# Sparse attention: value products of a pair's two heads on the two column halves of TensorE, compressed values as one product

## The chip, the core and the metric

One NeuronCore of one Trainium2 chip runs the whole program in one launch. The metric is the device time of that launch in microseconds (us). TensorE (PE) multiplies; its weight loads are shown as an engine of their own (PEld). VectorE (DVE), ScalarE (ACT) and GpSimd (POOL) work on the elements, and SyncE (SP) issues most of the DMAs.

## What is computed

The reference is a long chain of two blocks on 512 tokens of 1024 numbers: mixed attention and an expert layer in the first, a gated convolution and a sparse attention in the second. The change lies in the sparse attention at the end. Cut to that:

```python
p_c = masked_softmax(s_c, m_c)                       # over 31 compressed blocks
o_c = jnp.einsum('bqgin,bngd->bqgid', p_c, v_cmp)
...
p_s = masked_softmax(...)                            # selected blocks: 16 of 8, so all of them, causal
o_s = jnp.einsum('bqginl,bqgnld->bqgid', p_s, vg)
...
p_w = masked_softmax(s_w, m_w)                       # window of 512
o_w = jnp.einsum('bqgik,bkgd->bqgid', p_w, vw)
return g[..., 0:1] * o_c + g[..., 1:2] * o_s + g[..., 2:3] * o_w
...
y = o.reshape(B, S, ATTN_D) * jax.nn.silu(z)
return x + y @ w_out                                 # then a last norm
```

There are 16 heads of 64 in 4 groups of keys and values. With 512 tokens both the selected blocks and the window come to plain causal attention with keys and values of their own, two "branches".

## The kernel before

`phase_nsa` (from L1354) makes keys, values, compressed values, queries and gates, and then calls `attend` (L1632), where the change lies. Behind it comes the output product with `b_out` and the last norm.

`attend` works on pairs of heads: m is one of 8 pairs, which is 128 rows of the output, 64 for each head i. A job is (m, qb, i), with qb one of the four blocks of 128 queries in the order `QB = (3, 0, 2, 1)`; there are 64 jobs. Each passes through four steps, which `pipeline` records one job apart: `f_s` the scores of both branches (L1650 to L1652, the last being the mask as a bf16 product), `f_p` the softmax (maximum on DVE in L1662 or L1665, exponential on ACT in L1668, the sums' reciprocals and the scaling on DVE in L1669 to L1672), `f_t` the transposes on PE (L1681) and their copy to SBUF into `aT` on ACT (L1684), and `f_o` the products with the values (L1696, L1700).

`f_o` adds all terms of a pair into one PSUM bank `o` of 128 rows by 512 queries. A product of L1700 has 128 rows of keys, 64 columns of values and 128 queries, all in fp32, and writes 64 of the 128 rows of `o`: the lower half for i = 0, the upper for i = 1, which is also the half of the PE's columns on which it runs. Job (m, qb, i) has 2 (qb + 1) of these, all on one half. There are 320 of them in all, and each is two PE instructions in the trace (an fp32 product is made in two). Before the first of a pair's block stands L1696, the compressed values: 64 rows (two heads of 32 compressed keys each, and 32 pairs of pcT rows by the parity of m), 128 columns, 128 queries; 32 of these. When the last block of m is done, DVE multiplies `o` by the gate (L1704).

The names `s`, `pt`, `o` and `z` are banks of PSUM: four, two, one and one. The first stretch of `attend` has the last three of the gate's products (`z`, L178 to L180) laid between its jobs. The order on each engine is not the recorded one: a scheduler places the instructions by its own estimates, and each engine then runs its queue in order.

The compressed values `vbd` are laid out in `small_values` (L1489): four copies of 32 partitions each into a zeroed tile (L1366).

Of the kernel before, what the change touches and what calls it, by code (L numbers as in the profile page):

```python
# [10 lines left out]
F32 = mybir.dt.float32  # L11
# [7 lines left out]
PSUM = bass.MemoryType.PSUM  # L19
# [9 lines left out]
ND = 384  # tokens that go through all experts; the others fetch theirs  # L29

# how much of the work in the background is laid beside a unit of products, by part
# [4 lines left out]
# depths of the buffers  # L36
# [3 lines left out]
# where the products of a part turn to halves of the tokens, or are laid behind other work  # L40
# [4 lines left out]
# orders  # L45
# [12 lines left out]
class Ctx:  # L58
    """What all parts share: the core, the pools, the constants and the stream of weights."""
# [76 lines left out]
    def in_turn(self, op, prev=None):  # L136
        """Queue op behind prev, or behind the split that was traced last."""
        self.tc.add_manual_dep(op.ins, (prev or self.last).ins.name,
                               mybir.DependencyInfo(mybir.DependencyClass.NoSync, mybir.DependencyReason.DATA),
                               reason="pace")  # L140
# [41 lines left out]
    def gemm_w(self, key, out, act, k0=0, start=True, stop=True, pump=3.0):  # L182
        """out[m, t] (+)= sum over k of w[k, m] act[k, t] for one unit of weights."""
# [6 lines left out]
    def gemm_halves(self, jobs, act, done=None, after=None):  # L190
        """gemm_w on each half of the tokens in turn; jobs: (out, its units, each with its first k)."""
# [17 lines left out]
    def gemm_t(self, keys, outs, act, N, pump=3.0):  # L209
        """outs[tb][t, n] = sum over k of act[k, t] w[k, n]; keys: (unit, its first k, its count of k)."""  # L210
# [10 lines left out]
    def halves(self, hi, lo, src):  # L221
        """hi + lo = src exactly, each short enough for one pass."""
# [8 lines left out]
class Modulation:  # L231
    """silu(c) @ ada_w + ada_b, a sixth of its columns at a time, each a sum over rows and then partitions."""
# [33 lines left out]
def bcast(ap, n):  # L266
    """A row of DRAM on n partitions."""
    return bass.AP(tensor=ap.tensor, offset=ap.offset, ap=[[0, n]] + list(ap.ap))
# [33 lines left out]
class Norm:  # L302
    """1 / sqrt(mean of x^2 + eps) of each token, over all partitions; x [d, t] with d on partitions.

    The squares are summed with tokens on partitions, so that the root and its reciprocal (with a step of
    Newton's) take few elements, and brought back along the diagonal of a product."""
# [51 lines left out]
    def whole(self):  # L358
        """For all tokens at once, the squares summed by products."""
# [21 lines left out]
    def bare(self, k, g, act):  # L381
        """act = halves of x * g, their products to be scaled by r."""
# [7 lines left out]
def pipeline(n, stages, bg=None):  # L390
    """Emit stage s of job j at step j + s: later stages of earlier jobs first."""
# [10 lines left out]
# ================================================================ first block, mixing part  # L402
def phase_a(c, xres, mod):
    tc, nc, a = c.tc, c.nc, c.a
    with tc.tile_pool(name="pa", bufs=1) as pool, ExitStack() as scope, ExitStack() as pscope:
        psp = pscope.enter_context(tc.tile_pool(name="psa", bufs=7, space=PSUM))
        psm = pscope.enter_context(tc.tile_pool(name="psm", bufs=1, space=PSUM))
# [100 lines left out]
        def rotate(dsts, x, tab, tb, G):  # L508
            """x * cos + swap(x) * sin on G heads of 64."""
# [13 lines left out]
        def vt(keys, N, act_in):  # L523
            """A product with tokens on partitions."""
# [10 lines left out]
        def transposes(src, nblk, put):  # L535
            """src(b): [t, 128] to transpose; put(b0, n, psum) takes up to four of them."""
# [164 lines left out]
        # lambda  # L701
# [185 lines left out]
class Act:  # L887
    """The input of the products; its room is lent to the raw weights when it isn't needed."""
# [10 lines left out]
class Banks:  # L899
    """The eight banks of PSUM, taken in turn, or by the names that they are divided by."""  # L900
# [20 lines left out]
# ================================================================ experts  # L921
# [5 lines left out]
def phase_peer(c, xres, xscope, mod):  # L927
    """x += g2 * (sum over the chosen experts of gate * gelu(u . h) v).

    The first ND tokens go through all experts as products, their gates laid out over all experts (zero where  # L930
    an expert isn't chosen); the other tokens fetch the rows of their experts."""
# [10 lines left out]
    with ExitStack() as gscope, ExitStack() as psc, ExitStack() as vscope, ExitStack() as hscope, \  # L942
# [42 lines left out]
        def top16(vals, idx, src, tmp):  # L985
            """The 16 largest of a row, largest first, the earlier first among equals, and their places."""
# [89 lines left out]
        def gates(tb):  # L1076
            """The gate of every expert for each token: the sum over slots of one-hot x one-hot."""
# [35 lines left out]
        def gather():  # L1113
            """The experts of the tokens from ND on, a slot of all of them at a time."""
# [165 lines left out]
# ================================================================ second block: gated convolution  # L1280
# [72 lines left out]
# ================================================================ second block: attention  # L1353
# [499 lines left out]
```

## Time and profile before

| | us |
|---|---|
| median of 3 runs (2503.88 to 2516.2) | 2514.8 |
| span of the profiled execution, first to last instruction | 2495.9 |
| of it: attention, first product of `attend` to the last of L1700 | 222.4 |
| of it: from there to the end | 49.2 |

The span is the part of the profiled execution that the trace shows; what the launch takes around it is in the median of the runs alone. A record of a PE instruction starts when it is dispatched and ends when its results are written, so records overlap: the distance from one start to the next is what an instruction takes of the engine's time, and the chain of the profile is cut in just these distances. A line names the code, `o<-aT,V` is the tile written and the tiles read, and `128*64 128x128` is the rows and columns of the array and the moving operand.

### The profile page before, as it was taken

To read this page: it belongs to the slowest core of one execution; us is meant where nothing else is said; L and a number is where in the kernel's file an instruction comes from. 1 tells how busy PE (TensorE), PEld (TensorE's weight loads), DVE (VectorE), ACT (ScalarE), POOL (GpSimd) and SP (SyncE) were. 2 spreads that over 40 slices of the span, in tenths; PEclk is the share of its full clock that TensorE was granted. 3 is DMA by queue.
4 is the path that set the end of the run, shared out by engine and by line. 5 is a ranking of instruction groups with operands and counts; after the bars stand their busy time and mean duration, and the time that the engine had idled before them with its cause. 6 is when DMAs were issued, how large, how long until landed. Compare 5 with 4: busy or idle time off the path is not lost.

```text
span 2495.9 us, 37763 instructions
## 1 busy us (share of the span) xinstructions
PE 2461.3 (99%) x13725; PEld 2215.4 (89%) x13725; DVE 1861.5 (75%) x4173; ACT 1150.6 (46%) x2354; POOL 356.1 (14%) x332
## 2 busy tenths in 40 slices
PE   7999999999999999999999999999999999999998
PEld 4875788999999999999999999988888888887777
DVE  7885489999999878778888887765555456766654
ACT  3566443434777858633333333422222333545652
POOL 0000000014334333224332222000000010000000
PEclk8998999999999999999999999999999999999999
DMA  7560152468989998899999998332222352220002
GB/s 269 149 212 1 43 196 77 156 236 307 332 313 322 366 348 320 289 373 354 358 352 340 349 327 294 94 99 96 96 98 94 101 176 84 77 68 18 1 1 77
DMA packets 170939, 490.48 MB, mean 197 GB/s; under 512 B 15473, under 2 KB 62513, under 8 KB 169089
## 3 DMA queue, kind: packets, MB, share of 16 engines
q1 hardware_dynamic: 123744, 295.48, 34.3%
q0 software_dynamic: 44992, 189.68, 20.8%
q10 hardware_dynamic: 2016, 2.91, 0.4%
q8 instruction: 109, 1.79, 0.3%
q14 instruction: 78, 0.63, 0.1%
HBM read 437.15 MB, written 50.86 MB: 196 GB/s over the span
## 4 chain that ended last, share of the span: by engine, by line
PE 87%; DVE 5%; DMA 3%; issue 3%; POOL 1%; ACT 0%; SPq 0%; DVEq 0%; POOLq 0%; ACTq 0%
PE s L180 8%; PE s L179 8%; PE s L178 8%; PE mm L180 6%; PE mm L178 6%; PE mm L179 6%; PE pt L178 4%; PE pt L180 4%; PE pt L179 4%; PE gp L1081 3%; PE o L1700 3%; PE z L178 2%; PE z L180 2%; PE z L179 2%; PE o L180 2%
## 5 line engine op out<-in xcount | busy, mean ns | idle before, releaser
L102 ACT ACTIVATE whi<-wraw 128x1024 fp32r<-128x1024 f32 (+2 forms) x292 | 305.2, 1046 | 547.1 <-PE mm L179 167.2
L103 DVE TENSOR_TENSOR wlo<-wraw,whi 128x1024 fp32r<-128x1024 f32 (+2 forms) x292 | 350.6, 1202 | 97.7 <-ACT whi L102 96.0
L179 PE MATMUL mm<-act,whi 128*128 128x384 f32 (+2 forms) x1176 | 402.2, 343 | 0.0
L180 PE MATMUL mm<-act,wlo 128*128 128x384 f32 (+2 forms) x1176 | 401.5, 343 | 0.2
L178 PE MATMUL mm<-act,whi 128*128 128x384 f32 (+2 forms) x1176 | 398.9, 342 | 0.7 <-DVE xres L844 0.7
L102 ACT ACTIVATE whi<-act 128x1024 fp32r<-128x1024 f32 x126 | 133.5, 1060 | 324.9 <-issue 314.0
L180 PEld LDWEIGHTS mm<-act,wlo 128*128 128x128 f32 x1176 | 221.4, 188 | 5.4 <-DVE wlo L103 1.5
L179 PEld LDWEIGHTS mm<-act,whi 128*128 128x128 f32 x1176 | 221.4, 188 | 3.9
L178 PEld LDWEIGHTS mm<-act,whi 128*128 128x128 f32 x1176 | 219.8, 188 | 4.8 <-issue 0.8
L103 DVE TENSOR_TENSOR wlo<-act,whi 128x1024 fp32r<-128x1024 f32 x126 | 154.1, 1224 | 82.5 <-ACT whi L102 81.2
L1117 POOL DMA_INDIRECT ug<-in_peer_u_rows_dram,eiG x128 | 155.6, 1216 | 374.7 <-DVE ug L1125 258.9
L1117 POOL DMA_INDIRECT vg<-in_peer_v_rows_dram,eiG x128 | 158.6, 1239 | 295.6 <-DVE yG L1135 193.0
L179 PE MATMUL s<-w_lo,whi 128*128 128x384 f32 x512 | 171.1, 334 | 0.9 <-DVE w_lo L224 0.9
L178 PE MATMUL s<-w_hi,whi 128*128 128x384 f32 x512 | 170.3, 334 | 0.6 <-ACT ga L1191 0.6
L180 PE MATMUL s<-w_hi,wlo 128*128 128x384 f32 x512 | 170.5, 334 | 0.0
L1135 DVE SCALAR_TENSOR_TENSOR yG<-vg,gG,yG 128x1024 f32<-128x1024 f32 x127 | 162.2, 1277 | 7.4 <-DMA vg<-in_peer_v_rows_dram,eiG 7.2
L1125 DVE SCALAR_TENSOR_TENSOR ug<-ug,hG 128x1024 f32<-128x1024 f32 x128 | 155.4, 1217 | 8.7 <-DMA ug<-in_peer_u_rows_dram,eiG 8.6
L180 PE MATMUL s<-act,wlo 128*128 128x512 f32 x344 | 134.0, 390 | 0.2 <-DVE wlo L103 0.2
L178 PE MATMUL s<-act,whi 128*128 128x512 f32 x344 | 134.2, 391 | 0.0
L179 PE MATMUL s<-act,whi 128*128 128x512 f32 x344 | 133.6, 389 | 0.0
L1095 DVE TENSOR_SCALAR oh<-iof,idxT 128x128 f32<-128x128 f32 x384 | 116.7, 348 | 8.3 <-PE gp L1081 8.1
L1081 PE MATMUL gp<-oh,oh 128*128 128x128 f32 x768 | 115.0, 274 | 0.0
(676 smaller groups left out, 5810.4 us busy)
## 6 DMA issues: line engine op xcount, KB each, us to landing
wraw<-in_peer_u_dram SPq DMA_DIRECT2D x128, 512.0 KB, 5.3
act<-in_peer_v_rows_dram SPq DMA_DIRECT2D x126, 512.0 KB, 6.6
wraw<-in_a_in_dram SPq DMA_DIRECT2D x64, 512.0 KB, 3.3
Ad<-ga POOLq DMA_DIRECT2D x30, 768.0 KB, 8.2
ga<-Ad SPq DMA_DIRECT2D x30, 768.0 KB, 9.1
Gd<-gc POOLq DMA_DIRECT2D x10, 2048.0 KB, 10.2
gg<-Gd SPq DMA_DIRECT2D x32, 640.0 KB, 7.4
wraw<-in_ada_w_dram SPq DMA_DIRECT2D x32, 512.0 KB, 4.3
```

Source lines behind the costliest of these rows:

```text
L102: self.first = first = self.nc.scalar.activation(hi[:, :n], r[:, :n], AF.Copy)
L103: self.last = self.nc.vector.tensor_tensor(lo[:, :n], r[:, :n], hi[:, :n].bitcast(F32), op=OP.subtract)
L178: mm(out, lh, rh, start=start, stop=False)
L179: mm(out, lh, rl, start=False, stop=False)
L180: self.product = mm(out, ll, rh, start=False, stop=stop)
L1081: nc.tensor.matmul(gp[:, j, :], o1, o2, start=True, stop=True)
L1095: nc.vector.tensor_scalar(o1, iof, idxT[:, 0, t:t + 1], idxT[:, 2, t:t + 1], op0=OP.is_equal, op1=OP.mult)
L1117: nc.gpsimd.indirect_dma_start(out=t, out_offset=None, in_=tab, in_offset=bass.IndirectOffsetOnAxis(ap=eiG[:, j:j + 1], axis=0))
L1125: c.in_turn(nc.vector.scalar_tensor_tensor(u, u, 1.0, hG, op0=OP.mult, op1=OP.mult, accum_out=aG[:, j:j + 1]))
L1135: op = nc.vector.scalar_tensor_tensor(yG, v, gG[:, j:j + 1], yG, op0=OP.mult, op1=OP.add)
L1700: nc.tensor.matmul(o[rr, t], V[:, b, br * 256 + g * 64:br * 256 + (g + 1) * 64], ws[br][:, b * P:(b + 1) * P], start=False, stop=i == 1 an ...
```

## The change

`f_o` now does nothing for i = 0 but keep the transposed weights of the job; for i = 1 it issues the products of both heads, one of head 0, one of head 1 in turn. The ring `aT` has five tiles instead of four. The compressed values of a pair m are one product of 128 rows by 512 queries, whose weights `vbd[:, m % 2, g, :]` are zero in the rows that belong to the pair of the other parity; it opens the whole bank. `vbd` is zeroed and filled at the start of `attend` from a small tile `vsm`, which is one copy in `small_values`.

```diff
-        vbd = pool.tile([P, 4, P], F32, name="vbd")
+        vsm = pool.tile([P, 4, 64], F32, name="vsm")
         nc.gpsimd.memset(kbd, 0.0)
-        nc.gpsimd.memset(vbd, 0.0)
...
-            for q in range(4):
-                rr = slice(32 * q, 32 * q + 32)
-                cc = slice(64 * (q % 2), 64 * (q % 2) + 64)
-                nc.vector.tensor_copy(vbd[rr, :, cc], vv[rr, :, :])
+            nc.vector.tensor_copy(vsm, vv)
...
+    vbd = pool.tile([P, 2, 4, P], F32, name="vbd")
+    nc.gpsimd.memset(vbd, 0.0)
+    for q in range(4):
+        rr = slice(32 * q, 32 * q + 32)
+        nc.vector.tensor_copy(vbd[rr, q // 2, :, 64 * (q % 2):64 * (q % 2) + 64], vsm[rr, :, :])
...
-        ws, w1 = both(pool, "aT", n, bufs=4)
+        ws, w1 = both(pool, "aT", n, bufs=5)
...
     def f_o(j, ws):
         m, qb, i = jobs[j]
+        if i == 0:
+            held[m, qb] = ws
+            return
         g = m // 2
         t = slice(qb * P, (qb + 1) * P)
-        if i == 0 and qb == QB[0]:
+        if qb == QB[0]:
             O[m] = psp.tile([P, S], F32, name="o")
-        o = O[m]
-        if i == 0:
-            rr = slice(64 * (m % 2), 64 * (m % 2) + 64)
-            nc.tensor.matmul(o[:, t], vbd[rr, g, :], pcT[rr, g, t], start=True, stop=False, skip_group_check=True)
-        rr = slice(64 * i, 64 * i + 64)
+            nc.tensor.matmul(O[m], vbd[:, m % 2, g, :], pcT[:, g, :], start=True, stop=False, skip_group_check=True)
+        o, pair = O[m], (held.pop((m, qb)), ws)
         for br in range(2):
+            v = slice(br * 256 + g * 64, br * 256 + (g + 1) * 64)
             for b in range(qb + 1):
-                nc.tensor.matmul(o[rr, t], V[:, b, br * 256 + g * 64:br * 256 + (g + 1) * 64], ws[br][:, b * P:(b + 1) * P],
-                                 start=False, stop=i == 1 and br == 1 and b == qb, skip_group_check=True)
-        if i == 1 and qb == QB[-1]:
+                for h in range(2):
+                    nc.tensor.matmul(o[64 * h:64 * h + 64, t], V[:, b, v], pair[h][br][:, b * P:(b + 1) * P],
+                                     start=False, stop=br == 1 and b == qb, skip_group_check=True)
+        if qb == QB[-1]:
```

In the changed kernel's numbering the scores are L1651 to L1653, the transposes L1682, the compressed product L1700 and the value products L1706. On PE, at the turn to the third pair (m = 2), the queue before:

```order
L1681 MATMUL pt<-ident,aP 128x128 x4
L1696 MATMUL o<-pcT,vbd 128x128
L1700 MATMUL o<-aT,V 64x128 x8
L1650 MATMUL s<-Khi,Q 128x384
L1651 MATMUL s<-Klo,Q 128x384
L1652 LDWEIGHTS identb
L1652 MATMUL s<-maskb,identb 128x128
L1700 MATMUL o<-aT,V 64x128 x4
L1681 MATMUL pt<-ident,aP 128x128 x2
```

and the same place now:

```order
L1700 MATMUL o<-pcT,vbd 128x512
L1706 MATMUL o<-aT,V 64x128
L1682 MATMUL pt<-ident,aP 128x128 x8
L1651 MATMUL s<-Khi,Q 128x384
L1652 MATMUL s<-Klo,Q 128x384
L1653 LDWEIGHTS identb
L1653 MATMUL s<-maskb,identb 128x128
L1706 MATMUL o<-aT,V 64x128 x8
L1682 MATMUL pt<-ident,aP 128x128 x2
```

The 16 products of the block's two heads come in runs of 1, 8 and 7 now, where head 0 had one run of 8 and head 1 two of 4. Over all of `attend` the 320 products stand in 88 runs before and in 79 now; other work comes directly behind a run, or behind L1696, 95 times before, and 78 times behind a run now.

Inside a run the two heads alternate, which the tiles' numbers show; this is a run of 7 in the fifth pair (on PE, now):

```order
L1706 MATMUL o_22750<-aT_22730,V_20268 64x128
L1706 MATMUL o_22750<-aT_22697,V_20268 64x128
L1706 MATMUL o_22750<-aT_22730,V_20268 64x128
L1706 MATMUL o_22750<-aT_22697,V_20268 64x128
L1706 MATMUL o_22750<-aT_22730,V_20268 64x128
```

`aT_22697` holds head 0 and `aT_22730` head 1 of one block of queries; each row is two instructions in a trace. On DVE the four copies into `vbd` now stand at the start of `attend`, between the first maxima and the first sums:

```order
L1666 TENSOR_REDUCE amx<-s 128x1 x3
L1635 COPY vbd<-vsm 32x4x64 x4
L1670 RECIPROCAL asm<-asm 128x2
L1671 TENSOR_TENSOR asm<-asm,gates 128x2
L1673 TENSOR_SCALAR aP<-aP,asm 128x512 x2
```

Before, the reciprocal stood directly behind the three maxima. POOL's zeroing of `vbd` moved with them, behind the last weights of the small network and ahead of the DMAs that bring back `xres` for the output.

## Rows read from the trace of the kernel before

**Rows 1.** The page: the span, and PE's busy time, share and instructions.
```profile
span 2495.9 us, 37763 instructions
PE 2461.3 (99%) x13725; PEld 2215.4 (89%) x13725; DVE 1861.5 (75%) x4173; ACT 1150.6 (46%) x2354; POOL 356.1 (14%) x332
```

**Rows 2.** Busy time by stretch: length, then PE, PEld, DVE, ACT, POOL, clock, DMA.
```profile
2224.30:2446.70 222.40, 222.40 (x1519) 173.64 (x1518) 128.99 (x374) 123.86 (x367) 0.00 (x0) 1.00 0.03 11
2446.70:2495.90 49.20, 38.85 (x285) 36.31 (x285) 27.13 (x62) 14.44 (x28) 4.27 (x8) 0.94 0.29 97
```

**Rows 3.** The same view for one pair m in the middle of the attention.
```profile
2307.71:2332.26 24.55, 24.55 (x178) 19.26 (x177) 15.43 (x46) 14.77 (x47) 0.00 (x0) 1.00 0.00 1
```

**Rows 4.** Who waited for whom, 2224 to 2447: us in total, times, longest.
```profile
ACT aT L1684 <- PE pt L1681: 87.4, 76, 5.8
DVE amx L1662 <- PE s L1652: 30.6, 23, 1.9
...
PEld L1652 <- issue: 13.6, 63, 0.3
...
PEld o L1700 <- ACT aP L1668: 0.4, 1, 0.4
```

**Rows 5.** Groups by line, 2200 to 2450: busy us, mean ns, idle before and releasers.
```profile
L1700 PE MATMUL o<-aT,V 128*64 128x128 f32 x640 | 88.7, 280 | 0.0
L1700 PEld LDWEIGHTS o<-aT,V 128*64 128x64 f32 x640 | 67.5, 136 | 9.0 <-issue 3.0 <-ACT aP L1668 0.4
```

**Rows 6.** The chain of work, 2340 to 2352: start us, us, what.
```profile
2340.39 1.02 PE o L1700 x8
2341.41 0.58 PE pt L1681 x4
2342.00 0.18 PE s L1650
...
2344.46 0.45 PE pt L1681 x4
...
2345.77 0.42 PE o L1696 x2
2346.19 1.89 PE o L1700 x16
2348.08 0.37 PE s L1650
```

**Rows 7.** The chain at 2191: an fp32 product of 128 rows and 512 columns.
```profile
2191.45 0.86 PE o L1421 x2
```

**Rows 8.** PEld in order of time, the same run's weight loads, two and three of them.
```profile
2311.50 0.19 PEld L1700 LDWEIGHTS o<-aT,V 128*64 128x64 f32 x2
...
2311.50 0.30 PEld L1700 LDWEIGHTS o<-aT,V 128*64 128x64 f32 x3
```

**Rows 9.** PE in order of time, the products of these loads, one and two.
```profile
2311.51 0.32 PE L1700 MATMUL o<-aT,V 128*64 128x128 f32 x1
...
2311.51 0.43 PE L1700 MATMUL o<-aT,V 128*64 128x128 f32 x2
```

**Rows 10.** The zeroing of `vbd` and its copies: ns min/median/max, starts.
```profile
L1366 POOL MEMSET vbd<- x1: 525/525/525, 2028.8 to 2028.8; 128x512 f32 x1
...
L1489 DVE COPY vbd<-s x4: 406/420/429, 2130.7 to 2132.0; 32x256 f32<-32x256 f32 x4
```

**Rows 11.** DVE in order of time at the start of `attend`, and PE's first transposes.
```profile
2227.38 1.89 DVE L1665 TENSOR_REDUCE amx<-s 128x1 f32<-128x512 f32 x3
2229.64 0.17 DVE L1669 RECIPROCAL asm<-asm 128x2 f32<-128x2 f32 x1 [0.38 <-ACT aP L1668]
...
2233.55 0.88 PE pt L1681 x8
```

**Rows 12.** The chain behind the last value product.
```profile
2445.65 1.03 PE o L1700 x8
2446.70 1.07 ACT s L102
```

More of the change, by code (lines that the diff above doesn't have):

```diff
@@ L1599, in phase_nsa @@
         with tc.tile_pool(name="nsx", bufs=1) as p1:
-            attend(c, p1, psp, Q, Khi, Klo, V, vbd, pcT, gates, sz, gate)
+            attend(c, p1, psp, Q, Khi, Klo, V, vsm, pcT, gates, sz, gate)
         nscope.close()
@@ L1629, in phase_nsa, with attend @@
         qscope.close()
-def attend(c, pool, psp, Q, Khi, Klo, V, vbd, pcT, gates, sz, gate):
+def attend(c, pool, psp, Q, Khi, Klo, V, vsm, pcT, gates, sz, gate):
     nc = c.nc
     jobs = [(m, qb, i) for m in range(KD) for qb in QB for i in range(2)]
+    vbd = pool.tile([P, 2, 4, P], F32, name="vbd")
[3 more added lines that the diff above has]
+        nc.vector.tensor_copy(vbd[rr, q // 2, :, 64 * (q % 2):64 * (q % 2) + 64], vsm[rr, :, :])
     O = {}
@@ L1685, in f_t @@
         return ws
+    held = {}
     def f_o(j, ws):
         m, qb, i = jobs[j]
+        if i == 0:
+            held[m, qb] = ws
+            return
         g = m // 2
         t = slice(qb * P, (qb + 1) * P)
-        if i == 0 and qb == QB[0]:
+        if qb == QB[0]:
             O[m] = psp.tile([P, S], F32, name="o")
-        o = O[m]
-        if i == 0:
-            rr = slice(64 * (m % 2), 64 * (m % 2) + 64)
-            nc.tensor.matmul(o[:, t], vbd[rr, g, :], pcT[rr, g, t], start=True, stop=False, skip_group_check=True)
-        rr = slice(64 * i, 64 * i + 64)
+            nc.tensor.matmul(O[m], vbd[:, m % 2, g, :], pcT[:, g, :], start=True, stop=False, skip_group_check=True)
+        o, pair = O[m], (held.pop((m, qb)), ws)
         for br in range(2):
+            v = slice(br * 256 + g * 64, br * 256 + (g + 1) * 64)
             for b in range(qb + 1):
-                nc.tensor.matmul(o[rr, t], V[:, b, br * 256 + g * 64:br * 256 + (g + 1) * 64], ws[br][:, b * P:(b + 1) * P],
-                                 start=False, stop=i == 1 and br == 1 and b == qb, skip_group_check=True)
-        if i == 1 and qb == QB[-1]:
+                for h in range(2):
+                    nc.tensor.matmul(o[64 * h:64 * h + 64, t], V[:, b, v], pair[h][br][:, b * P:(b + 1) * P],
+                                     start=False, stop=br == 1 and b == qb, skip_group_check=True)
+        if qb == QB[-1]:
             y = pool.tile([P, S], F32, name="y", bufs=2)
```

## The prediction

> **What bounds the kernel now.** I read the page first: PE is busy for 99% of the span, no other engine over 75% [rows 1]. A mean over such a long program says little of one stage, so I cut the attention out by stretches: for 222.40 us, from its first score product to its last value product, PE is busy without a gap, at a granted clock of 1.00, while DVE has 128.99 us of work and ACT 123.86 [rows 2]. One pair m in the middle takes 24.55 us, with 15.43 of DVE and 14.77 of ACT [rows 3]. Busy PE need not be PE that sets the pace, so the waits come next: ACT waits 87.4 us for the transposes, DVE 30.6 for scores, and PE waits for nobody, but for 0.4 us in all; what is left of its idle time is "issue", 0.3 us at the longest [rows 4]. So the stage lasts as long as PE's queue takes to run. The next instructions behind it hang on its end: a split of `b_out` on ACT begins at 2446.70, when the last value products have ended [rows 12]. What the stage gains should reach the end of the program.
>
> **What an instruction takes.** A group's mean of 280 ns [rows 5] is a record's length, not its cost. The chain gives costs: a run of 8 value instructions takes 1.02 us and one of 16 takes 1.89, so 8 more cost 0.87, which is 0.109 each; 1.02 less 8 x 0.109 leaves 0.15 for each run, whatever its length [rows 6]. The work behind a run pays too: four transposes take 0.58 behind value products and 0.45 behind scores, 0.13 more, and a score product takes 0.37 where it otherwise takes 0.18 [rows 6]; I take 0.14. So going to a run of half-array products and back costs 0.29, about 0.145 each way. The compressed product pays the same twice over: L1696's 128 columns take 0.42 [rows 6], of which two instructions of 0.107 stream, if an fp32 product of 512 columns takes 0.86 [rows 7] and so 0.215 for 128.
>
> **The change part by part.**
>
> 1. *Fewer switches.* The runs go from 88 to 79, which is 9 x 0.15 = 1.3 us less. The 32 products of L1696 cost 32 x 0.42 = 13.4 us; the 8 that replace them have 128 rows and 512 columns, 0.86 each by [rows 7], 6.9 us, and need no switch: 6.5 us less. Returns to the whole array go from 95 to 78: 17 x 0.14 = 2.4 us less. Together 10.2 us, all of it in PE's queue, with nothing beside it. This needs no overlap and comes whatever the next part does. The multiplied zeros cost nothing, since 8 x 512 columns stream as long as 32 x 128.
>
> 2. *Two halves in turn.* Now 640 instructions take 640 x 0.109 = 69.8 us. No row shows two products on different halves next to each other, so this is bounded from both sides. Best: the second instruction of one head's product streams beside the first of the other's. A run of n products then takes n + 1 steps of 0.109 instead of 2n, and the saving is (320 - 79) x 0.109 = 26.3 us. Worst without a new cost: no overlap, 0. Between them: the loads. A load's record is 0.136 long and a product's 0.28 [rows 5]. The second load of a run begins 0.054 behind the first (0.19 less 0.136) and the third 0.164 behind it (0.30 less 0.136) [rows 8], just when the second product has begun, at 0.15 (0.43 less 0.28) [rows 9]. So a load goes out when the instruction ahead of it has started, and on one half it is then hidden. If the load for the other half also waits for that start, each change of half shows these 0.053 or so and a product of two instructions takes 0.109 + 0.053 = 0.162 instead of 0.218: 241 x 0.056 = 13.5 us. Below zero: if each change of half is paid like a switch of shape, 241 x 0.145 = 35 us are lost. I take the best end: the two streams need different columns, different rows of `o` and different tiles `aT`, the weights of the other half are free to be loaded, and the tie of load to start in [rows 8] is seen only where the half in question is in use.
>
>    [...]
>
> 3. *The start of `attend`.* POOL zeroes `vbd`, twice the size of the old one, 0.53 us for that [rows 10], so some 1.05. The only thing behind it on POOL are the DMAs of `xres`, which wait for the end of the attention anyway. Then DVE makes four copies, 4 x 0.42 = 1.7 us [rows 10], behind the first three maxima and ahead of the first sums. DVE's first sums waited 0.38 for ACT, and the scaled weights are done at about 2231, while PE's first transposes begin at 2233.55 [rows 11]: 1.3 us later is still in time. The compressed product waits for these copies, and stands ahead of the first transposes. Cost 0, up to 1.7 if the zeroing is late. In `small_values` three copies (1.3 us of DVE) go from a stretch in which PE is full; 0.
>
> 4. *What holds the products back.* The lower head's weights wait for the upper's, and `aT` has five tiles, of which a pair of the larger blocks takes four. In the order the earlier pair's products stand ahead of every transpose that reuses their tiles, so this is 0 on paper. But the gain brings DVE and ACT nearer to PE: 36.5 us less is 4.6 per pair, 20.0 of 24.55, and DVE is then busy for 15.43 / 20.0 = 77% and ACT for 74%. They still fit, but the handoffs that PE never waited for get shorter, and the order was made by estimates that I don't know. I take 3.5 us for waits that appear (a tenth of the gain; a choice). From 0 to 8.
>
> **Sum.** 10.2 + 26.3 - 3.5 = 33 us. The profiled span goes from 2495.9 to about 2463. The median of the runs is 18.9 over the span and the lowest 8.0 [rows 1], so I carry the difference over: 2514.8 - 33 = 2482 us.
>
> **The rivals.**
>
> A. *Loads aren't pulled ahead.* The halves overlap only in part, for what [rows 8] shows on one half holds across halves. 10.2 + 13.5 - 2 for waits = 22 us: 2493 us. For it: the load always leaves just behind the start of the instruction ahead. Against: that is also what two places for weights per half would give.
>
> B. *The change doesn't do what it says.* PE's queue is strict and a product waits for the one ahead, half or no half: only the switches go. 10 us: 2505 us; if also every change of half shows a load, 241 x 0.053 = 12.8 are lost and it is 2517. For it: no record here shows two products streaming at once. Against: nothing but the absence.
>
> [...]
>
> [...]
>
> **How the numbers follow.** Forecast 0.43, A 0.27, B 0.20, C 0.10. A measurement of this kernel tells about 0.5% from no change, 12.6 us; the three runs of before are 12.3 us apart. Faster by more than that: the forecast, A, and few cases of B with luck in the order: 0.74. Within: most of B, and C where its price is small: 0.17. Slower: 0.09. The range has to take in the forecast, with no waits at 2514.8 - 36.5 = 2478 and some room for the spread of the runs below it, A at 2493, and the main case of B at 2505: 2475 to 2506 leaves out C and the worse half of B, a little under 0.2.
>
> **What the profile of the changed kernel would show.** In a run of 7 or 8 value products the chain or the starts: 0.109 per product (two instructions) for the forecast, 0.162 for A, 0.218 for B, 0.36 for C. The stretch of the attention at about 190 us for the forecast, 201 for A, 212 for B. Runs of one product at some 0.37 (two instructions of 0.109 and 0.15). The compressed product at 0.86, eight of them. Waits of PE for `aP`, `aT` or for maxima that were not there before, some us in all: over 10 would say that part 4 was too small and that DVE or ACT took over. PE waiting at the first compressed product for `vbd` would say that part 3 was wrong. A stretch behind the attention that isn't 49 us would say that the gain does not pass through to the end.

## The result, and the profile after

The changed kernel takes 2465.2 us (median of 4 runs, 2458.9 to 2476.5) beside 2514.6 us for the kernel before (4 runs, 2503.9 to 2516.2): a ratio of 0.9836, 95% interval 0.9808 to 0.9864. It is faster, as forecast, but the time lies below the range of 2475 to 2506. So the question is where some 17 us more than the 33 of the sum came from.

The profiled execution of the changed kernel has a span of 2467.7 us and took 2469.45. The stretches of the attention and of what follows, in the columns of [rows 2] (length, then busy time of PE, PEld, DVE, ACT and POOL, granted clock, DMA):

```profile
2230.00:2416.20 186.20, 186.20 (x1476) 138.12 (x1474) 126.14 (x378) 122.07 (x367) 0.95 (x1) 1.00 0.04 13
2416.20:2467.70 51.50, 39.63 (x283) 37.26 (x282) 27.10 (x62) 14.42 (x28) 4.27 (x8) 0.90 0.27 93
```

From the first score product to the end of the last value product the attention went from 222.30 us (the window of [rows 2] is 0.1 wider) to 186.18, 36.1 less, and PE is busy for all of it, as in [rows 2]. DVE and ACT have the work they had, now 68% and 66% of the stretch. Who waits for whom in it, in the columns of [rows 4]:

```profile
ACT aT L1685 <- PE pt L1682: 54.1, 57, 4.2
DVE amx L1666 <- PE s L1653: 19.9, 32, 3.5
DVE amx L1663 <- PE s L1653: 15.2, 20, 1.8
...
PEld o L1706 <- ACT aP L1669: 1.5, 6, 0.4
```

ACT and DVE still wait for PE (54.1 us where it was 87.4 in [rows 4]). In the other direction only weight loads wait, 3.2 us in all, of which the last row is the largest; PE itself has no gap. What a run of value products takes is read from the chain of work, as in [rows 6] (start, us, engine, tile, line, count of instructions, two of which are a product):

```profile
2284.71 0.81 PE o L1706 x12
...
2286.66 0.80 PE o L1706 x10
...
2290.02 1.02 PE o L1706 x14
...
2292.52 0.91 PE o L1700 x2
...
2295.24 1.02 PE o L1706 x16
...
2404.39 0.36 PE o L1706 x2
...
2415.19 1.03 PE o L1706 x14
2416.25 1.07 ACT s L102
```

The ends of PE's records are modelled by the profile, so no row shows when results are written, and the pieces of a chain run from one end to the next, not from start to start; for a whole run it comes to the same: in the first row the 12 start at 2284.64, and what follows them starts at 2285.45. Sixteen instructions take 1.02 us, as eight did in [rows 6], and 14 take the same. The last row is the split of `b_out` on ACT, which begins at the attention's end as in [rows 12].

That two products stream at once is seen in the rows of PE in order of time. These are three answers for one run, cut 0.03, 0.26 and 0.37 us after its start; a row counts what had started by the cut:

```profile
2264.47 0.33 PE L1706 MATMUL o<-aT,V 128*64 128x128 f32 x2
...
2264.47 0.44 PE L1706 MATMUL o<-aT,V 128*64 128x128 f32 x4
...
2264.47 0.55 PE L1706 MATMUL o<-aT,V 128*64 128x128 f32 x6
```

Where single instructions followed each other in [rows 9], pairs do now. In the records of this run the two of a pair start 6 or 7 ns apart.

**What the 17 us are.** The runs of the kernel before, 70 more of them beside the experiments, have a median of 2504.7 us (2495.1 to 2519.9); only 9 of the 70 are at 2514.4 or above, where three of the first four lay. The 70 come from four chips, whose medians lie between 2503 and 2506, so it is not the chip that makes the difference, as far as is known (that of the first runs is not on record). Twenty runs of the changed kernel have a median of 2468.8 us (2456.1 to 2477.9). In every run the time is its span plus 1.7 to 1.85 us. The distance to the forecast is then: 10.1 us because the median of the three runs it started from was that much above the median of many, 2.9 because the gain is 35.9 us and not 33, and 3.6 because the first four runs of the changed kernel were that much below their own median of many; 16.6 in all.

The spread of a kernel's runs follows the granted clock. At a mean clock of 0.987 to 0.989 the spans of before average 2495.6 us (24 runs), at 0.983 to 0.985 2503.8 (24), at 0.979 to 0.981 2512.8 (22); those of the changed kernel 2458.8 (7), 2468.0 (9) and 2474.5 (4). The difference is 36 to 38 us at each level. Where the clock is lost is seen in the first fifth of the program. The stretch from 180 to 240 us in the trace of before, in the columns of [rows 2]:

```profile
180.00:240.00 60.00, 60.00 (x257) 34.89 (x257) 32.84 (x90) 37.22 (x136) 0.00 (x0) 0.77 0.03 9
```

the same in that of the changed kernel:

```profile
180.00:240.00 60.00, 60.00 (x194) 32.15 (x193) 27.56 (x77) 30.06 (x112) 0.00 (x0) 0.60 0.03 9
```

and in that of `e4_turn_only`, one of the experiments below:

```profile
180.00:240.00 60.00, 60.00 (x166) 31.92 (x166) 25.56 (x71) 27.21 (x103) 0.00 (x0) 0.53 0.03 9
```

The instructions up to there are the same in all three, yet PE got through 257, 194 and 166 of them. In the trace of before the clock is 0.50 from 184 to 208 us and 1.00 from 210 to 240, in that of the changed kernel 0.50 from 182 to 228 and 1.00 from 229 to 240. If it has only these two values in the stretch, a mean of 0.77 is 27.6 us at 0.50 and the rest at 1.00; 0.60 is 48 us, and 0.53 is 56.4 us with more to come. In each of the three PE had been idle for 0.69 us at 177 us, waiting for ACT, and some 3 to 5 us later the clock fell: it is 0.68 from 180 to 182 us in the changed kernel, and 0.55 and 0.63 from 182 to 186 in the other two. In the chain of the changed kernel that wait is

```profile
176.71 0.25 PE ps L180
176.96 0.02 issue
176.98 0.61 ACT act L531
177.59 0.04 issue
177.63 0.49 PE s L734 x2
```

The gap goes with the fall, but it does not explain it. At 285 us PE waits 1.41 us for DVE, twice as long, and the clock stays at 1.00, here in the changed kernel:

```profile
280.00:300.00 20.00, 18.51 (x101) 15.56 (x100) 9.73 (x13) 11.13 (x21) 0.00 (x0) 1.00 0.24 78
```

It is so in the six profiles that have these stretches, the two of before, two of the changed kernel, `e3_no_turn` and `e4_turn_only`: from 120 to 180 us PE is idle for 0.69, from 180 to 200 the clock is 0.50 to 0.58, and in the 20 us that hold the longer gap, between 260 and 300, PE is idle for 1.49 and the clock is 1.00. How long it stays down differs: 27.6, 48 and over 60 us in the three traces, in which the attention starts at 2224.4, 2230.0 and 2239.6 us.

### The profile page after: what moved, and what is told of

The parts are those of the page before. It is cut to its first block, busy times and chain, and to the rows that moved or that the text cites. A ratio compares the mean times of both kernels' runs of the same rounds, so it can differ in the third digit from the quotient of the medians.

```text
span 2467.7 us, 37681 instructions
## 1 busy us (share of the span) xinstructions
PE 2432.1 (99%) x13677; PEld 2183.5 (88%) x13677; DVE 1857.9 (75%) x4174; ACT 1149.0 (47%) x2354; POOL 354.0 (14%) x332
## 4 chain that ended last, share of the span: by engine, by line
PE 93%; DMA 3%; DVE 3%; issue 0%; ACT 0%; SPq 0%; DVEq 0%; ACTq 0%
PE mm L178 8%; PE mm L180 8%; PE mm L179 8%; PE s L180 8%; PE s L179 8%; PE s L178 8%; PE pt L178 4%; PE pt L180 4%; PE pt L179 4%; PE gp L1081 3%; PE z L178 2%; PE z L179 2%; PE z L180 2%; PE o L1706 2%; PE o L178 2%; PE o L179 2%
```

## The experiments

The attention's length, from its first score product to the end of its last value product, turned out to be independent of the clock's draw earlier on: 222.30 us in both profiles of the kernel before, 186.17 to 186.18 in four of the changed kernel. So it is the number to compare; the ratio of the whole stands beside it. Ratios are against runs of the kernel before in the same rounds. "Steps" is worked out from the queue: in each run, twice the number of products on the half that has more of them. That is what a run takes if the halves overlap fully, as they do not in `e10_one_then_other` (28.5 steps for a run's 16, below).

| kernel | runs of products | steps | attention, us | median, us (runs) | ratio to before, 95% interval |
|---|---|---|---|---|---|
| before | 88 | 640 | 222.30 | 2504.7 (70) | 1 |
| changed | 79 | 384 | 186.18 | 2468.8 (20) | see below |
| `e3_no_turn` | 95 | 634 | 217.14 | 2497.8 (10) | 0.9974 (0.9949 to 0.9998) |
| `e4_turn_only` | 80 | 384 | 195.54 | 2486.0 (6) | 0.9924 (0.9888 to 0.9960) |
| `e5_whole_runs` | 50 | 356 | 174.24 | 2456.7 (5) | 0.9803 (0.9778 to 0.9828) |
| `e7_by_two` | 81 | 448 | 193.62 | 2475.7 (4) | 0.9871 (0.9844 to 0.9899) |
| `e8_fixed_steps` | 34 | 324 | 201.78 | 2490.7 (6) | 0.9915 (0.9885 to 0.9945) |
| `e9_last_first` | 32 | 320 | 167.50 | 2456.4 (6) | 0.9797 (0.9757 to 0.9837) |
| `e12_last_first_again` | 32 | 320 | 167.51 | 2449.6 (6) | 0.9792 (0.9767 to 0.9817) |
| `e10_one_then_other` | 32 | 320 | 189.88 | 2472.2 (4) | 0.9865 (0.9820 to 0.9911) |

**The two kernels again.** `e1_after_again` is the changed kernel, `e2_before_again` the kernel before.

> The changed kernel again, beside the kernel before. Theory (the attention gained 36.4 us, 222.40 to 186.00, and the rest of the difference between the first medians, 49.5 us, is a granted clock that fell early in the program in some executions): at one mean granted clock the two spans differ by 36 to 38 us, the medians by 34 to 45, and the attention lasts 186 us again. Rival (the change gains some 12 us more somewhere outside the attention): the spans differ by 47 to 50 us also where the mean clocks are equal. Second question: what lies around the span. Theory: each run is its span plus 1.7 to 1.8 us, so 2459 to 2475. Rival, the one the prediction carried: 8 to 19 us over the span.

> The kernel before against itself. Theory: the same, ratio 1.000 within 0.004; its spans lie between 2495 and 2515 and follow the mean granted clock, 0.01 of clock being some 20 to 25 us, and the time is the span plus 1.75 us in each run. The attention lasts 222.4 us whatever the clock did earlier. Rival (the profiled execution of before, 2495.9, is a thing of the profiler, and runs without it need 2503 or more at the same clock): spans of 2503 to 2515 at a mean clock of 0.988.

The changed kernel: attention 186.18 us, median 2470.4, ratio 0.9864 (0.9828 to 0.9900); at clocks of 0.988 and 0.989 its spans were 2461.8 and 2454.4, on average some 37 below those of before at that clock. The medians differ by 33.0, a little less than the 34 to 45 that were expected. The kernel before against itself: 1.0011 (0.9984 to 1.0038), attention 222.30, spans 2494.4 to 2517.1 with the clock from 0.989 down to 0.979, each 1.7 to 1.8 us below its time. So there is no gain elsewhere, and the profiled execution of before was an ordinary one with a high clock.

Two later repeats asked whether the change itself moves the clock.

> The changed kernel a third time, on the chip and in the rounds of the two kernels above. Theory: the attention lasts 186.2 us again; the start of the attention lies at 2221 to 2240 us, the later the lower the mean granted clock (2222 at 0.988, 2230 to 2235 at 0.984), and the time is that start plus 186.2, plus 49 to 52 for the rest, plus 1.75. Rival (the change itself lowers the clock): starts at 2230 and later in all its runs, where those of before stay at 2224.

> The changed kernel in the same rounds. Theory: the attention lasts 186.2 us, the ratio to before is 0.985 to 0.986 where the clocks are drawn alike ((2504.7 - 36.1) / 2504.7 = 0.9856), and the kernel with 32 whole runs lies 18 to 19 us below it. Rival (clocks differ by kernel): a ratio outside 0.983 to 0.988.

They gave 0.9833 (0.9790 to 0.9876) and 0.9862 (0.9836 to 0.9888), attention 186.18 and 186.17. The four profiled executions of the changed kernel all have a clock of 0.983 or 0.984 and begin the attention at 2228.9 to 2235.0, which alone would suit the rival. But over all runs the mean clock is 0.9846 (20 runs) beside 0.9843 for before (70), and 7 of the 20 have 0.987 or more, as 24 of the 70 do. So the rival falls: the clock's draw is not the change's doing. One of these expectations was missed by a little: the kernel with 32 whole runs (below) lies 19.7 us under `e13_after_fourth` by the medians, for 18 to 19.

**Without the turn.** All products of head 0, then all of head 1:

```diff
-        for br in range(2):
-            v = slice(br * 256 + g * 64, br * 256 + (g + 1) * 64)
-            for b in range(qb + 1):
-                for h in range(2):
+        for h in range(2):
+            for br in range(2):
+                v = slice(br * 256 + g * 64, br * 256 + (g + 1) * 64)
+                for b in range(qb + 1):
```

> As the changed kernel, but a block's products are issued all of head 0, then all of head 1, so that a change of half comes once in a run, not at every product. Theory (the two streams overlap only where neighbours are on different halves): a run of n products takes 2n steps of 0.109 us, less one where it changes half, so about 26 us of the gain are lost; the queue has 95 runs here against 79, which at 0.29 each adds some 4.6: the attention lasts 213 to 217 us, +26 to +31 us against the changed kernel, -5 to -10 against before. Rival (the gain comes from the merged block, the larger compressed product and the fifth tile of aT, and not from the turn): the attention stays at 186 to 192 us.

The attention took 217.14 us, 30.96 more than the changed kernel, at the upper end of what was expected, and 5.16 less than before. In its queue a run stays on one half, with one exception, and the chain shows what that costs:

```profile
2300.95 0.58 PE o L1706 x4
...
2304.15 0.80 PE o L1706 x6
...
2311.70 0.36 PE o L1706 x2
```

Six instructions take 0.80 us here; in the changed kernel twelve do. The turn is the change's main part, and the rival that credits the rest falls.

**Only the turn.** The compressed values as before, 32 products of 64 rows with the old layout of `vbd`:

```diff
-            nc.tensor.matmul(O[m], vbd[:, m % 2, g, :], pcT[:, g, :], start=True, stop=False, skip_group_check=True)
+        rr = slice(64 * (m % 2), 64 * (m % 2) + 64)
+        nc.tensor.matmul(O[m][:, t], vbd[rr, g, :], pcT[rr, g, t], start=True, stop=False, skip_group_check=True)
```

> As the changed kernel, but the compressed values as before: 32 products of 64 rows, one per block of a pair, with the tile vbd laid out as before; the heads still go in turn. Theory: the 8 large products cost 8 x 0.86 = 6.9 us where the 32 cost 32 x 0.42 = 13.4, and each of the 32 that is followed by other work pays a return of 0.14: +7 to +10 us, the attention at 193 to 196, about -27 us against before. Rival (the small product, on 64 of the 128 rows, also breaks the pairing of the two heads behind it, or the array's shape goes through more states): +12 us or more. Other rival (the switch is paid once per run in any case, and the small product opens a run that would be opened anyway): +0 to +3 us.

195.54 us, 9.36 more: within the 7 to 10, so both rivals fall. Its median, 2486, says little, since four of its six runs drew a clock of 0.979 to 0.981; the one at 0.987 has a span of 2466.5, 7.7 above the mean of the changed kernel's seven at 0.987 to 0.989.

**Every second change of half.** Two products of one head, then two of the other:

```diff
-        for br in range(2):
-            v = slice(br * 256 + g * 64, br * 256 + (g + 1) * 64)
-            for b in range(qb + 1):
-                for h in range(2):
+        todo = [(br, b) for br in range(2) for b in range(qb + 1)]
+        for k in range(0, len(todo), 2):
+            for h in range(2):
+                for br, b in todo[k:k + 2]:
+                    v = slice(br * 256 + g * 64, br * 256 + (g + 1) * 64)
```

> The changed kernel, but the heads change after every two products, not after every one: two of head 0, two of head 1, and so on; 81 runs. Theory (only the instructions next to a change of half stream beside each other, and one change hides one step of 0.109): a run of n products then shows about 88 hidden steps in all instead of 241, so 16.7 us of the overlap are lost and some 0.8 for two runs more: the attention at 203 to 204 us. Rival (the two halves are queues of their own, and PE runs ahead on the one while the other is busy, so the grain of the turn doesn't matter): 186 to 190 us. Other rival (only a strict alternation pairs at all): 213 to 217, as with no turn.

193.62 us, 7.4 more and not 16.7: the theory that each change hides one step falls. The chain:

```profile
2316.80 0.58 PE o L1707 x4
...
2318.00 1.07 PE o L1707 x16
...
2320.11 1.02 PE o L1707 x12
```

Sixteen instructions in blocks of four by half take 1.07 us, nearly as in strict turn (1.02). As I read it, PE does not keep to the order of its queue here: it passes the instructions that wait for the busy half and starts those of the free one. The run of 16, cut 0.07 us after its start, has two instructions under way, and the four at its head are all of one half:

```profile
2317.93 0.34 PE L1707 MATMUL o<-aT,V 128*64 128x128 f32 x2
```

The row with 12 is four products on one half and two on the other: 0.15 + 8 x 0.109 = 1.02, the fuller half alone. What the kernel loses are runs of two products of one head, 31 of them, at 0.58: in all 64 steps more, 64 x 0.109 = 7.0 us, and two runs. The rival of two queues was right in kind; its 186 to 190 had not counted those runs.

**How far PE gets ahead.** The kernel with whole runs (below), but in each run all products of head 1 and then all of head 0:

```diff
-        for br in (1, 0):
-            v = slice(br * 256 + g * 64, br * 256 + (g + 1) * 64)
-            for b in range(qb + 1):
-                for h in (1, 0):
+        for h in (1, 0):
+            for br in (1, 0):
+                v = slice(br * 256 + g * 64, br * 256 + (g + 1) * 64)
+                for b in range(qb + 1):
```

> As the kernel with 32 whole runs, but inside a run all products of head 1 come first and then all of head 0, so that there is one change of half in a run. It asks how far PE gets ahead on one half while the other is busy. Theory 1 (each half is a queue without a bound that matters here): a run of 16 products lasts 1.9 us as with the turn, and the attention 165 us. Theory 2 (PE looks past a few instructions only; two products, four instructions, were passed in the kernel that changes by two): in each run four steps are hidden, the run of 16 products lasts 3.2 us, and the attention 165 + 34.9 - 14 = 186 us. Theory 3 (one hidden step at the change): 3.5 us, and 196 us.

189.88 us. The chain has its four kinds of runs, of 2, 6, 4 and 8 products for each head:

```profile
2321.25 0.59 PE o L1706 x8
...
2326.05 2.38 PE o L1706 x24
...
2330.44 1.51 PE o L1706 x16
...
2336.46 3.26 PE o L1706 x32
```

3.26 us is 0.15 and 28.5 steps for 32 instructions, 1.51 is 12.5 steps for 16, and 0.59 is 4 for 8: a change of half hides four steps less at most a half. In order of time, the run of 32, cut 0.06, 1.33, 1.83 and 3.21 us in:

```profile
2336.39 0.32 PE L1706 MATMUL o<-aT,V 128*64 128x128 f32 x1
...
2336.39 1.52 PE L1706 MATMUL o<-aT,V 128*64 128x128 f32 x12
...
2336.39 2.02 PE L1706 MATMUL o<-aT,V 128*64 128x128 f32 x20
...
2336.39 3.33 PE L1706 MATMUL o<-aT,V 128*64 128x128 f32 x32
```

Twelve instructions one by one, eight in the next half microsecond, and then twelve one by one again. The last four of head 1 stream beside the first four of head 0. Theory 2 stands, and theories 1 and 3 fall. Its 186 us started from 165 for the whole runs, which take 167.5 (below), and three of the four kinds of run hide 3.5 steps and not 4, another 1.3 us.

**Fewer runs.** First, a block's first product queued behind head 1's last copy:

```diff
-            nc.scalar.activation(dst, src, AF.Copy)
+            copied[j] = nc.scalar.activation(dst, src, AF.Copy)
...
+                    if first:
+                        c.in_turn(op, copied[j])
+                        first = False
```

> The changed kernel with a block's first value product placed in PE's queue behind head 1's last copy into aT, so that a block's 16, 4, 12 or 8 products stand in fewer pieces: 50 runs in place of 79, as 9, 7 / 4 / 7, 5 / 8 in most pairs. Theory (a run costs 0.15 when it opens, 0.14 behind it and one step of 0.109 in which only one half streams, 0.399 in all): 29 runs fewer are 11.6 us, the attention at 174.6 us against 186.2; DVE with 126 us of work and ACT with 122 still fit. Rival (the order of the changed kernel spends those switches to cover waits: products held back until all copies are done leave PE without work while ACT copies): the attention at 186 us or more, with waits of PE for aT, aP or amx of over 10 us.

174.24 us, 11.9 less, as expected, with no gap on PE, so the rival falls here. Then the transposes and scores held to a fixed order as well:

```diff
+            if "o" in last:
+                c.in_turn(op, last["o"])
...
+                if "o" in last:
+                    c.in_turn(op, last["o"])
...
                         c.in_turn(op, copied[j])
+                        c.in_turn(op, last["s"])
```

> As the kernel with fewer pieces, and the transposes and scores recorded behind a block's products are also queued behind the last of them, and the products behind the last score recorded before them: every block's products are one run, 34 runs in all instead of 79. Theory (0.399 for each run, and no waits): 45 x 0.399 = 18.0 us, the attention at 168 us. Rival (with the order fixed step by step, a block's transposes follow only 16 to 4 products and one or two scores behind their softmax, so PE waits for ACT's exponentials and DVE's scaling): waits of PE for aP and aT of 5 us and more, the attention at 174 to 190 us, at or above the kernel with 50 runs.

201.78 us: the rival holds, and its upper end was still too low. PE is busy for 183.05 of them, and the waits are there:

```profile
2220.60:2422.40 201.80, 183.05 (x1474) 137.87 (x1472) 129.69 (x378) 120.26 (x367) 0.95 (x1) 0.99 0.04 12
```

```profile
PEld pt L1684 <- ACT aT L1689: 18.4, 26, 0.9
...
PEld o L1711 <- ACT aT L1689: 10.3, 17, 1.6
PE pt L1684 <- DVE aP L1675: 7.6, 13, 0.7
...
PE o L1711 <- ACT aT L1689: 6.2, 17, 1.4
```

Last, nothing but the order of issue turned round, so that a block's first product needs what is copied last:

```diff
-        for br in range(2):
+        for br in (1, 0):
...
-                for h in range(2):
+                for h in (1, 0):
...
-                                     start=False, stop=br == 1 and b == qb, skip_group_check=True)
+                                     start=False, stop=br == 0 and b == qb, skip_group_check=True)
```

> The changed kernel with a block's products issued from the other end: branch 1 ahead of branch 0 and head 1 ahead of head 0, so that the first product reads the tile aT that ACT copies last. By that alone all products of a block stand in one run: 32 runs of 16, 4, 12 and 8 in place of 79, each with as many products on one half as on the other. Theory (a run lasts 0.15 + 0.109 for each instruction on the fuller half, and 0.15 is paid behind it): steps of 0.109 fall from 384 to 320, 7.0 us, and 47 runs fewer at the 0.307 that the kernel with 50 runs showed are 14.4 us: the attention at 164.8 us, against 174.2 with 50 runs and 186.2 in the changed kernel; DVE and ACT are then busy for three quarters. Rival (the whole run waits for the last copy, as in the kernel with fixed steps): waits of PE for aT, aP or pt of 5 us or more, and the attention at 170 to 200 us.

> The kernel with 32 whole runs again. Question: five of its six executions had a mean granted clock of 0.984 or less, and four of them 0.979 to 0.981. Theory (the stretch of half clock ahead of the attention is a draw of each execution, whatever the kernel): over this run's executions the clock lies between 0.979 and 0.989 as for before (mean 0.984 in 59), the attention lasts 167.5 us again, and the ratio to before is near (2504.7 - 54.8 + 1) / 2504.7 = 0.978 to 0.979. Rival (this kernel draws the lower clock more often): again 0.979 to 0.981 in most executions, a start of the attention at 2235 or later, and a ratio of 0.980 or more.

167.50 us, and 167.51 in the repeat: 18.7 below the changed kernel, with PE busy for all but 0.2 us.

```profile
2238.40:2405.90 167.50, 167.30 (x1476) 131.81 (x1474) 124.98 (x378) 118.94 (x367) 0.95 (x1) 1.00 0.04 14
```

```profile
2320.58 0.59 PE o L1706 x8
...
2325.37 1.46 PE o L1706 x24
...
2328.83 1.02 PE o L1706 x16
...
2334.36 1.90 PE o L1706 x32
```

Each run is 0.15 and half its instructions at 0.109. This kernel beats both: 0.9792 (0.9767 to 0.9817) of the time of before. As I read it, the scheduler lays other work where it estimates a wait, and finds none inside a run whose first product is the last to be ready. The 2.7 us to the expected 164.8 are the price of a run: from the changed kernel to this one, 18.7 less 64 x 0.109 = 7.0 leaves 11.7 for 47 runs, 0.25 each, where the step to 50 runs had shown 0.307. Its clock was 0.979 to 0.984 in five of six runs, 0.982 to 0.985 in the repeat; the mean of the twelve is 0.9827 beside 0.9843 for before, which 12 runs are too few to call a difference, so this stays open.

## The prediction, step by step

**What bounds the kernel** was right: PE's queue sets the attention's length in every kernel but the one with the fixed steps, and what it gained went through to the end, but for about 1.5 us. The stretch behind the attention, which was to stay at 49 us, was 49.25 and 49.85 in the two profiles of before and 51.5, 49.4, 50.2 and 52.7 in those of the changed kernel. It goes with one transfer, of the last `b_out` weights, which stands in the chain there. The profiled execution has:

```profile
2418.59 8.86 DMA wraw<-in_b_out_dram
...
2427.58 0.85 issue
```

In the order of the lengths above it takes 6.98 and 7.58 us in before, and 8.86, 7.05, 7.93 and 9.69 in the changed kernel. The stretch less the transfer is 42.3 in four of the six, and 42.6 and 43.0 in the two with the longest. In these two PE stood without work behind the transfer, and the clock fell for 3.4 us (0.57 from 2430 to 2434 in the profiled one, 0.72 from 2434 to 2440 in `e13_after_fourth`, each 3.4 us if it fell to 0.50). Why the transfer takes longer in some executions wasn't tried, nor whether the change has a part in it.

**Fewer switches** (step 1) was forecast at 10.2 us. By the steps below, 256 x 0.109 = 27.9 of the 36.1 us are the overlap, which leaves 8.2. The chain of work, added up by line over the attention, says where they came from. The value products fell from 82.6 to 53.4 us, 29.2 less: the 27.9, and the 1.3 of nine runs fewer. The compressed products fell from 12.9 to 7.2 us, 5.7 less where 6.5 was forecast; five of the eight stand directly behind a mask product and take 0.91, as in the chain above, and not 0.86. All other work of PE gave 1.2 where the returns were to give 2.4; 0.7 of that difference are three instructions of the output's product, 0.23 each, which the new order puts ahead of the last run, so that they only moved from one stretch to the other. The 9.4 of `e4_turn_only` belong to another queue: in it a score product follows 21 of the 32 small products, where in before it was 7. The price of a run, 0.29 in the sum, is 0.25 over 47 runs (0.31 over the 29 of `e5_whole_runs`).

**Two halves in turn** (step 2) was forecast at 26.3 us, the best end of its bounds, and that end was right; the formula was not quite. A run of n products does not take n + 1 steps but as many as the fuller half needs: 14 and 16 instructions both take 1.02 us, 10 and 12 both 0.80. So an odd run is as the formula has it and an even one saves a step more: 384 steps and not 399, 1.6 us. The premise, that only neighbours overlap, was wrong as well, though it cost nothing here: `e7_by_two` overlaps with four instructions of one half in a row.

Rival A's 22 us would have come if a load for the other half had shown its 0.053 us at each change. The runs disagree: 16 instructions with their 16 loads take 1.02 us, which is 0.15 and eight steps of 0.109.

**The start of `attend`** (step 3) was rightly costed at 0. POOL's zeroing took 0.95 us (1.05 estimated), the four copies 1.19 (1.7 estimated), and the first compressed product came three microseconds behind them:

```profile
2234.85 1.19 DVE L1635 COPY vbd<-vsm 32x256 f32<-32x256 f32 x4
```

```profile
2239.22 0.91 PE o L1700 x2
```

**What holds the products back** (step 4) was forecast at 3.5 us and is none: PE has no gap in 186.2 us. The prediction had noted that the order keeps earlier products ahead of every transpose that reuses their tiles and that DVE would be busy for 77%; it is 74% from 2274 to 2393 us, in the middle pairs from which the figure was taken, and 68% over the whole, since among other things DVE has only 2.6 us of work in the last 16.2, where the output's products stand. The allowance was a choice with no row behind it. Even at 167.5 us, with DVE at 75%, there were 0.2 us of gaps. What makes PE wait is the order, as `e8_fixed_steps` shows with hardly any change in DVE's and ACT's work.

**The base** is the step that failed. "The median of the runs is 18.9 over the span" was read as a thing to carry over. Around the span there are 1.75 us; the other 17 were the distance between one execution with a clock of 0.988 and three that, by their times, had less (their clocks are not on record). Some 7 of the 17 were right to carry, for the median of 70 runs is 8.8 over that span; the other 10.1 were the draw of three runs. The range had no room for them: its lower end lies 3 us under the sum without any waits, where the three runs alone were 12.3 apart. From the median of 70 runs the sum would have given 2471.7 us, and what is left to 2465.2 are the 2.9 and 3.6 above.

At like clock the sum can be tested without any draw. From the profiled execution it gives 2495.9 - 33 + 1.75 = 2465 us at a clock of 0.988, and 2459.1 + 1.8 = 2460.9 was measured there. So the sum itself was some 4 us too small, about what it had taken off for waits that didn't appear. That 2465 is also the median of the first four runs is chance, for their clocks go from 0.981 to 0.988.

**The rivals** all fall: A's 0.162 and B's 0.218 for a product have no row, since 0.109 is measured, and C, in which each change of half is paid like a change of shape, 0.145 us, is excluded by 241 changes of half that cost nothing: 1.02 us for 16 instructions that change half at each product, as for eight on one half in [rows 6]. What fills the 0.25 us that a run costs beside its streaming, no row shows.

## What to carry to other kernels

Here two streams of small products on different halves of the array (fp32, 128 rows, 64 columns, 128 moving columns) cost only what the longer of them costs where the half changes after every two or four instructions of the queue: 1.02 and 1.07 us for 16, where eight on one half take 1.02. With all 16 of one half ahead of the other's, 32 took 3.26 us in place of 1.90. What is left is the price of going to the half-array shape and back, 0.25 us a run over 47 runs, so group the products into long runs, for instance by issuing first the one whose operand is ready last. Make a sum against the span of the profiled execution, and compare spans at like clock: a median of three runs can lie 10 us off, and a stage's length, which at a granted clock of 1.00 is here the same to 0.02 us from run to run, tells in one profile what ten runs of the whole program don't.

## What the runs showed of the hardware

The overlap of the two column halves in fp32 was complete where they alternate: 16 instructions take 1.02 us, as eight on one half did [rows 6]. And by the starts, PE took instructions of the free half ahead of their turn in the queue. In the run of 16 in `e7_by_two` the second start comes within 0.07 us of the first; a record doesn't name its half, but instructions of one half start 0.109 us apart or more, so this one is of the other, and three for the busy half stand ahead of it in the queue. No run shows it going further: in the run of 32 of `e10_one_then_other` twelve start one by one in 1.33 us and eight in the next half microsecond, so the first pair of starts comes with the 13th of the 16 instructions of head 1, when three of them are still to start. So four steps were hidden at most: 3.5 in the run of 32, which takes 3.26 us, all four in the run of 8, which takes 0.59. Whether PE picks from one queue or has a short one for each half, no run tells apart.

In the three traces shown the granted clock falls from 1.00 to 0.50 between 180 and 184 us, behind a gap of 0.69 us on PE, and stays there, with PE busy throughout, for 27.6 us, for 48 and for over 60. What sets it off and what decides how long was not found: behind a gap of 1.41 us some 100 us later the clock stayed at 1.00. The times of one kernel follow their mean clock: the kernel before had spans of 2495.6 us on average at 0.987 to 0.989 and of 2512.8 at 0.979 to 0.981.
